# Fifteenth mixing gate ahead of the first S5 states, one input product ahead of the first S5 output and a third one behind the last

## The chip, the cores and the metric

The kernel runs on one core of one Trainium2 chip. The metric is the device time of one execution in microseconds (us), taken as the median of a few runs. A core has five engines with one in-order instruction queue each: PE (TensorE, the matrix products), DVE (VectorE), ACT (ScalarE), POOL (GpSimd) and SP (SyncE, which here only issues transfers). They wait for one another through semaphores.

## What is computed

One layer of a recurrent diffusion backbone for 128 context tokens and 512 latent tokens, 640 columns in all. Cut to what matters here:

```
hn = rmsnorm(x) * (1 + sc1) + sh1
xa, ga, xs = split(hn @ w_in, [1024, 2048])          # LRU input, LRU gate, S5 input
ua = depthwise_conv4(xa)                             # centred, per channel
r, i = sigmoid(block_diag(ua, w_r) + b_r), sigmoid(block_diag(ua, w_i) + b_i)    # per direction
ha = linear_scan(a(r), b(r, i, ua)), both directions
ya = gelu(ga) * ha
vs = gelu(S5(xs) + D * xs);  ys = vs * sigmoid(vs @ s5_w_glu + b)
gate_a, gate_b = split(sigmoid(hn @ w_gate + b_gate))
m  = (gate_a * (ya @ w_proj_lru) + gate_b * (ys @ w_proj_s5)) @ w_out
x  = x + g1 * rmsnorm(m);   then a SwiGLU feed-forward part
```

## The kernel before

Every matrix product is done in three passes over operands split into a high and a low part, so one product of a 128-column weight block with the 640 columns of `hn` is 48 matmuls (8 blocks of the inner dimension, 3 passes, 2 halves of the columns). The weights are cut into units that stand in one list. For each unit SP fetches a raw tile (`raw`, 4 buffers), ACT writes the high part (`wh`) and DVE the low part (`wl`, 3 buffers each). `use` and `split_next` do this on demand, two units ahead of the product that is being written down; the next raw tiles are fetched as `wl` frees them. So the position of a unit in the list and the position of its product in the code both set what stands where in the queues of SP, ACT and DVE.

The order of the work is written by hand; each engine executes its instructions in the order in which the Python code emits them. The stretch of this study is the middle of the layer:

- The gate loop (products 2 to 13 of `w_gate`, `gate_job`) runs on PE while DVE walks through the 64 steps of the S5 state scan (`scan_step`, tile `F`). The steps lie in a list of background jobs, and `bg_run` emits some after each gate. `mod_done` at gate 12 puts a few DVE instructions behind the scan steps that are emitted by then: the first of them writes `modT` from the PSUM tile `q_m2`.
- `gate_job(m)` is a product into the PSUM tile `q_g`, a `shift` copy, two sigmoids on ACT and a store (`gd`) that ACT issues. PSUM has four such tiles (`q`), used in turn by every product.
- After the scan, `y_states(ct)` copies states out of `F` into two `Hst` tiles (six copies on DVE, six on ACT), for one of four channel tiles `ct`. `y_mm` multiplies with them (PSUM `q_y`), `y_out` transposes (`q_yt`) and applies GeLU on ACT (tile `vs`). Between `y_mm` and `y_out` of each `ct` one product of the LRU branch stands: `lru_xa(0)`, `lru_xa(1)`, `lru_ga(0)`, `lru_ga(1)`. An `lru_xa` is followed by `lru_x`, which copies the result to a padded tile (`xap`).
- Then come four products of the S5 gate (`glu_job(0..3)`, PSUM `q_glu`, each half as long as an input product). Behind the second and the fourth the depthwise convolution of LRU block 0 and 1 is emitted on DVE (`lru_conv`, tile `u`, and its parts `uh`, `ul`). Then `softplus` (26 tiny DVE instructions on 16 columns, tile `w16`), then `lru_w(0)` and `lru_w(1)`, which split the LRU gate weights into `lwh` (ACT) and `lwl` (DVE).
- Then a loop over pairs of blocks `c` = 2, 4, 6: two input products, the LRU gate products of the two blocks before (`lru_gates`, PSUM `q_gl`, which needs `uh`, `ul`, `lwh` and `lwl`), two more products of the other half (`lru_ga`), and the LRU recurrences on ACT and DVE.

Of the kernel before, what the change touches and what calls it, by code (L numbers as in the profile page):

```python
# [18 lines left out]
KD = D // 128  # L19
# [20 lines left out]
def hybrid_step_kernel(ctx: ExitStack, tc: tile.TileContext, A, y_prompt, y_sample, o_lru, o_re, o_im):  # L40
# [23 lines left out]
    def mm(out, lhsT, rhs, start, stop):  # L64
        PE.matmul(out, lhsT=lhsT, rhs=rhs, start=start, stop=stop, skip_group_check=True)  # L65

    def psq(name):
        return ps.tile([128, 1024], F32, tag="q", name=name)

    def ttile(name, shape=(128, TW), dt=F32, pool=None):  # L70
        return (pool or tp).tile(list(shape), dt, tag="t", name=name)
# [4 lines left out]
    def bg_run(us=1e9, upto=None):  # L76

        credit[0] = us if upto or us > 1e8 else credit[0] + us
        while bg and credit[0] > 0:
            if upto and upto not in [job for _, job in bg]:  # L80
                break
            cost, job = bg.popleft()
            if callable(job):
                job()
            credit[0] -= cost
        if upto or not bg:
            credit[0] = 0.0
# [33 lines left out]
    def unit(src, shape, split=True):  # L121
        units.append({"src": src, "shape": list(shape), "split": split})
        return len(units) - 1
# [67 lines left out]
    def colmajor(w, c0, n=128):  # L191
        return w[:, c0:c0 + n].rearrange("(k p) c -> p k c", p=128)

    w_in, w_gate, w_mod = A["w_in"][0], A["w_gate"][0], A["w_mod"][0]
# [16 lines left out]
    U_XA, U_GA = [], []  # L211
    U_GLU = None
    for c in range(0, 8, 2):
        for j in range(2):
            U_XA.append(unit(colmajor(w_in, (c + j) * 128), (128, KD, 128)))
        for j in range(2):
            U_GA.append(unit(colmajor(w_in, 1024 + (c + j) * 128), (128, KD, 128)))
            if c + j == 1:
                U_GLU = [unit(w_glu[:, m * 256:m * 256 + 256].rearrange("(k p) c -> p k c", p=128), (128, 4, 256))
                         for m in range(2)]  # L220
    U_G.append(unit(colmajor(w_gate, GO[15] * 128), (128, KD, 128)))
# [100 lines left out]
    q = psq("q_c")  # L322
# [44 lines left out]
    q = psq("junk")  # L367
# [172 lines left out]
    def vec(name, i):  # L540
        o = VOFF[name] + i
        return V[:, o:o + 1]
# [95 lines left out]
    for k in range(KD + 1):  # L638
        if k < KD:
            q = psq("q_x")  # L640
# [130 lines left out]
    def seg_act(out, q, func, b):  # L771
        for s, (lo_, hi_) in enumerate(((0, NP), (NP, T))):
            act(out[:, lo_:hi_], q[:, 192 + lo_:192 + hi_], func, bias=b[:, s:s + 1])
# [17 lines left out]
    xq = [psq(f"q_xs{m}") for m in range(2)]  # L791
# [32 lines left out]
    q = psq("q_xs")  # L824
# [15 lines left out]
    def gate_mm(m):  # L840
        q = psq("q_g")
        mtile(q, wblocks(U_G[m]), hn, range(KD))
        return q

    def gate_job(m, pool=None, q=None):
        q = gate_mm(m) if q is None else q
        g = ttile("gate", pool=pool)
        seg_act(g, q, AF.Sigmoid, shift(q, vec("b_gate", GO[m])))
        if pool is None:
            ACT.dma_start(out=gd[GO[m]], in_=g[:, 0:T])  # L850
        return g[:, 0:T]
# [119 lines left out]
    def y_load(ct, half):  # L971
        tk = ttile("tk")
        g0 = 8 * ct + 4 * half
        for g in range(4):
            b = Kd[g0 + g, 0:16, 0:8 * H5]
            SP.dma_start(out=tk[:, g * 128:(g + 1) * 128],
                         in_=bass.AP(tensor=b.tensor, offset=b.offset, ap=[[H5, 8]] + list(b.ap)))
        return tk
# [8 lines left out]
    q = gate_mm(0)  # L987
# [31 lines left out]
    for m in range(2, 14):  # L1019
# [10 lines left out]
        if 5 <= m < 13:  # L1030
# [2 lines left out]
            k_stage(m - 5)  # L1033
            bg_run(2.2)
    tks = [y_load(0, 0), y_load(0, 1)]
    bg_run()


# [26 lines left out]
    def y_mm(ct, tks, Hst):  # L1065
        ysb = [ttile(f"ysb{a}") for a in range(2)]
        for half in range(2):
            tk = tks[half]
            g0 = 8 * ct + 4 * half
            q = psq("q_y")  # L1070
            for gg in range(4):
                g = g0 + gg
                o = q[0:NCH, gg * 128:(gg + 1) * 128]
                mm(o, Ug(g), tk[:, gg * 128:(gg + 1) * 128], True, False)
                for d in range(2):
                    hs = Hst[d][:, (g % 8) * NCH:(g % 8 + 1) * NCH]
                    mm(o, hs, Pt[d][:, g].rearrange("p k h -> p (k h)"), False, d == 1)
            for a in range(2):
                src = q[0:NCH, 0:512].rearrange("p (g j h) -> p j g h", g=4, j=8)[:, ::-1][:, 4 * a:4 * a + 4]
                dst = ysb[a][0:NCH, 0:512].rearrange("p (j g h) -> p j g h", j=4, g=8)[:, :, 4 * half:4 * half + 4]  # L1080
                if a:
                    act(dst, src, AF.Copy)
                else:
                    DVE.tensor_copy(out=dst, in_=src)
        return ysb
# [26 lines left out]
    def lru_xa(c):  # L1112
        q = psq("q_xa")
        mtile(q, wblocks(U_XA[c]), hn, range(KD))
        return q
# [3 lines left out]
    def lru_x(c, q):  # L1119
        x = ttile("xap", pool=lps[-1])  # L1120
        POOL.memset(x[:, 0:2], 0.0)
        POOL.memset(x[:, 130:133], 0.0)
        POOL.memset(x[:, 645:648], 0.0)
        b = shift(q)
        act(x[:, 2:130], q[:, 192:320], AF.Identity, bias=b[:, 0:1])
        act(x[:, 133:645], q[:, 320:832], AF.Identity, bias=b[:, 1:2])
        return x
# [27 lines left out]
    def lru_ga(c, ahead=2):  # L1155
        q = psq("q_ga")
        mtile(q, wblocks(U_GA[c], ahead=ahead), hn, range(KD))
        return q

    def lru_gelu(c, q):  # L1160
        g = ttile("gel")[:, 0:T]
        seg_act(g, q, AF.Gelu_apprx_tanh, shift(q))
        gel[c] = g
# [85 lines left out]
    fin = ttile("fin")  # L1249
    DVE.tensor_copy(out=fin[:, 0:64].rearrange("p (a b) -> p a b", a=2), in_=F[:, :, :, 16])  # L1250
    hst = y_states(0)
    gate_job(14)
    xs0 = []
    for ct in range(4):
        ysb = y_mm(ct, tks, hst)
        if ct == 0:
            q = psq("q_ns")
            transpose(q[0:64, 0:128], fin[:, 0:64])
            fo = ttile("fin")
            DVE.tensor_copy(out=fo[0:64, 0:128], in_=q[0:64, 0:128])  # L1260
            SP.dma_start(out=o_re[0, 0].rearrange("d (g a) p -> (d g) (a p)", a=2), in_=fo[0:32, 0:128])
            SP.dma_start(out=o_im[0, 0].rearrange("d (g a) p -> (d g) (a p)", a=2), in_=fo[32:64, 0:128])
        if ct < 3:
            tks = [y_load(ct + 1, 0), y_load(ct + 1, 1)]
            hst = y_states(ct + 1)
        xq = lru_xa(ct) if ct < 2 else lru_ga(ct - 2)
        y_out(ct, ysb)
        if ct < 2:
            xs0.append(lru_x(ct, xq))
        else:  # L1270
            lru_gelu(ct - 2, xq)
    fp.__exit__(None, None, None)
    s5p.__exit__(None, None, None)
    lpool = tc.tile_pool(name="lru", bufs=27, side="right")
# [15 lines left out]
    def glu_job(m):  # L1290
        q = psq("q_glu")
        mtile(q, wblocks(U_GLU[m // 2], 4, (m % 2) * 128), vsh, range(4))
        g = ttile("sg")[:, 0:T]
# [11 lines left out]
    for c in range(2):  # L1305
        lru_w(c)
    for c in range(2, 8, 2):
        q = lru_xa(c)
        if c > 2:
            lru_scan(c - 4)  # L1310
        xs = [lru_x(c, q)]
        q = lru_xa(c + 1)
        if c > 2:
            lru_scan(c - 3)
            lru_mul(c - 4)
            lru_mul(c - 3)
        lru_conv(c, xs[0])
        xs.append(lru_x(c + 1, q))
        lru_gates(c - 2)
        lru_gates(c - 1)  # L1320
        lru_conv(c + 1, xs[1])
        gq = [lru_ga(c)]

        def front():
            lru_iu(c - 2)
            lru_iu(c - 1)
            for j in range(2):
                lru_ul(c + j)
            for j in range(2):
                lru_w(c + j)  # L1330
            gq.append(lru_ga(c + 1, ahead=1))

        def s5_split():
            for m, g in enumerate(yf):
                yh = ttile(f"ysh{m}", dt=F32R)[:, 0:T]
                yl = ttile(f"ysl{m}", dt=F32R)[:, 0:T]
                act(yh, g, AF.Copy)
                tt(yl, g, yh, ALU.subtract)
                ys.append((yh, yl))
            split_next()  # L1340

        if c < 6:
            ta = lru_decay((c - 2, c - 1), front, split_next)
        else:
            ta = lru_decay((c - 2, c - 1), None, lambda: [front(), s5_split()])
        lru_drive(ta, (c - 2, c - 1))
        if c > 2:
            lru_split(c - 4)
            lru_split(c - 3)
        for j in range(2):  # L1350
            (lru_gelu if c < 6 else lru_raw)(c + j, gq[j])
        warm(AF.Sigmoid)
# [89 lines left out]
    for j, (part, m) in enumerate(items):  # L1442
        if j:
# [5 lines left out]
            elif part == "b":  # L1449
                for i in range(NP1):  # L1450
                    q = psq("q_pl")
# [5 lines left out]
            else:  # L1457
                q = psq("q_pl")
# [7 lines left out]
        if j == 2:  # L1466
            q = psq("q_nl")
# [86 lines left out]
    for i in range(5):  # L1554
# [3 lines left out]
        q = wo_mm(i, mid)  # L1558
# [88 lines left out]
    for k in range(KH):  # L1647
        a, b = tk[k]
        p, q = f[k], f[k + KH]
# [206 lines left out]
```

## Time and profile before

| | us |
|---|---|
| median of 3 runs | 1039.13 (1036.62 to 1042.95) |
| the profiled execution, its own time | 1037.07 |
| its span in the trace | 1035.3 |
| PE busy | 989.7 (96% of the span) |
| PE weight loads busy | 911.1 (88%) |
| DVE busy | 668.3 (65%) |
| ACT busy | 461.0 (45%) |
| POOL busy | 197.2 (19%) |

PE is the engine that is nearly always busy; the other four work beside it. The busy share is a mean over stages, so what a reordering is worth is read from the few places where PE waits, and from what ends each wait.

### The profile page before, as it was taken

The page shows a single profiled execution, that of the slowest core. Times are in us where ns is not written, and L with a number is a line of the kernel's source. Part 1 is how long each engine was busy: PE and PEld are TensorE (multiplying, and loading weights), DVE is VectorE, ACT ScalarE, POOL GpSimd, SP SyncE. Part 2 cuts the span into 40 slices and gives each one's busy share as a digit, 9 for nine tenths or more (in the row PEclk, how much of TensorE's full clock was granted, in tenths as well). Part 3 has the DMA queues.
Part 4 walks back from the last instruction along what each step waited for, and adds up shares of the span by engine and source line. Part 5 has one row for each costly group of instructions (what it writes and reads, how often), then busy time and mean ns, then how long its engine had stood idle before and what let it go on. Part 6 is the DMA issues. An engine that isn't in the chain of part 4 may idle for free.

```text
span 1035.3 us, 16728 instructions
## 1 busy us (share of the span) xinstructions
PE 989.7 (96%) x6649; PEld 911.1 (88%) x6649; DVE 668.3 (65%) x1103; ACT 461.0 (45%) x748; POOL 197.2 (19%) x200
## 2 busy tenths in 40 slices
PE   5999999979999999999999989999999999999997
PEld 3698988879999999987877889999999999888885
DVE  5789899962477989782575785555555565434113
ACT  5535423234349889732242443444454454333112
POOL 4000000000000000300310274555555551000002
PEclk9999999989999999999999999999999999999999
DMA  9944276543213221747562312223322223522202
GB/s 305 322 115 128 68 210 199 186 152 96 63 42 102 61 73 49 259 133 210 178 201 104 121 43 82 81 83 87 96 83 82 83 82 122 206 79 82 70 13 101
DMA packets 135901, 125.57 MB, mean 121 GB/s; under 512 B 17320, under 2 KB 115384, under 8 KB 135824
## 3 DMA queue, kind: packets, MB, share of 16 engines
q1 hardware_dynamic: 129888, 111.82, 35.1%
q10 hardware_dynamic: 4080, 7.31, 2.1%
q0 software_dynamic: 1856, 5.38, 1.5%
q8 instruction: 52, 0.85, 0.3%
q14 instruction: 25, 0.20, 0.1%
HBM read 111.63 MB, written 12.85 MB: 120 GB/s over the span
## 4 chain that ended last, share of the span: by engine, by line
PE 73%; DVE 15%; ACT 5%; DMA 3%; issue 2%; SPq 0%; POOL 0%; ACTq 0%; DVEq 0%
PE f L65 15%; PE ffX L65 13%; PE q_g L65 6%; PE ffY L65 6%; PE q_pl L65 6%; PE q_xa L65 4%; PE q_wo L65 3%; PE ffZ L65 3%; PE q_ga L65 3%; DVE wl L59 2%; PE q_ff L65 2%; PE q_y L65 2%; PE q_m L65 2%; PE q_gl L65 2%; DVE F L59 2%
## 5 line engine op out<-in xcount | busy, mean ns | idle before, releaser
L59 DVE TENSOR_TENSOR wl<-raw,wh 128x1024 fp32r<-128x1024 f32 (+1 forms) x104 | 126.5, 1221 | 148.9 <-ACT wh L62 148.7
L62 ACT ACTIVATE wh<-raw 128x1024 fp32r<-128x1024 f32 (+1 forms) x106 | 110.5, 1047 | 180.2 <-PE f L65 81.9
L59 DVE TENSOR_TENSOR wl<-s,wh 128x1024 fp32r<-128x1024 f32 x38 | 55.1, 1450 | 60.8 <-ACT wh L62 60.8
L65 PE MATMUL f<-wl,ah 128*128 128x512 f32 x220 | 87.1, 396 | 0.0
L65 PE MATMUL f<-wh,ah 128*128 128x512 f32 x220 | 87.1, 396 | 0.0
L65 PE MATMUL f<-wh,al 128*128 128x512 f32 x220 | 87.1, 396 | 0.0
L65 PE MATMUL q_g<-hnh,wh 128*128 128x320 f32 (+1 forms) x256 | 60.8, 319 | 5.5 <-ACT Hst L62 5.5
L59 POOL TENSOR_TENSOR s<-raw 128x512 f32<-128x512 f32 x38 | 52.6, 1384 | 58.1 <-DVE wl L59 30.0
L65 PE MATMUL q_g<-hnl,wh 128*128 128x320 f32 (+1 forms) x256 | 59.4, 313 | 0.0
L65 PE MATMUL q_g<-hnh,wl 128*128 128x320 f32 (+1 forms) x256 | 59.3, 314 | 0.0
L65 PEld LDWEIGHTS f<-wl,ah 128*128 128x128 f32 x220 | 41.5, 188 | 9.9
L65 PEld LDWEIGHTS f<-wh,al 128*128 128x128 f32 x220 | 41.4, 188 | 10.0
L65 PEld LDWEIGHTS f<-wh,ah 128*128 128x128 f32 x220 | 41.4, 188 | 9.9
L65 PEld LDWEIGHTS q_g<-hnh,wh 128*128 128x128 f32 x256 | 43.5, 192 | 6.9 <-ACT Hst L62 5.7
L65 PE MATMUL ffX<-Th,wh 128*128 128x320 f32 x152 | 47.0, 310 | 0.0
L65 PE MATMUL ffX<-Tl,wh 128*128 128x320 f32 x152 | 47.0, 310 | 0.0
L65 PE MATMUL ffX<-Th,wl 128*128 128x320 f32 x152 | 47.0, 309 | 0.0
L62 ACT ACTIVATE u<-ffX 128x320 f32<-128x320 f32 x38 | 16.6, 438 | 64.3 <-PE ffX L65 64.3
L62 ACT ACTIVATE wh<-s 128x1024 fp32r<-128x1024 f32 x38 | 39.8, 1048 | 11.4 <-PE q_ff L65 6.0
L65 PEld LDWEIGHTS q_g<-hnl,wh 128*128 128x128 f32 x256 | 43.8, 192 | 0.0
L65 PEld LDWEIGHTS q_g<-hnh,wl 128*128 128x128 f32 x256 | 43.8, 191 | 0.0
L59 DVE TENSOR_TENSOR F<-F,sc 128x64 f32<-128x64 f32 (+1 forms) x128 | 39.5, 308 | 3.8
(388 smaller groups left out, 2803.9 us busy)
## 6 DMA issues: line engine op xcount, KB each, us to landing
raw<-in_w_ff_in SPq DMA_DIRECT2D x44, 512.0 KB
raw<-in_w_mod SPq DMA_DIRECT2D x32, 512.0 KB
raw<-in_w_ff_out SPq DMA_DIRECT2D x22, 512.0 KB
raw<-in_w_in SPq DMA_DIRECT2D x20, 512.0 KB
raw<-in_w_gate SPq DMA_DIRECT2D x16, 512.0 KB
wm<-in_w_mod SPq DMA_DIRECT2D x12, 512.0 KB
gd<-gate ACTq DMA_DIRECT2D x16, 320.0 KB
raw<-in_w_out SPq DMA_DIRECT2D x8, 512.0 KB
```

The source lines that it names most:

```text
L59: (eng or DVE).tensor_tensor(out=out, in0=a, in1=b, op=op)
L62: ACT.activation(out=out, in_=in_, func=func, **kw)
L65: PE.matmul(out, lhsT=lhsT, rhs=rhs, start=start, stop=stop, skip_group_check=True)
```

## The change

The product of gate 14, with its evacuation, is emitted before the background list is run empty and so before the copy `fin` and `y_states(0)`; it stood behind both. The first input product, `lru_xa(0)` with `lru_x(0)`, moves from between `y_mm(0)` and `y_out(0)` to the place ahead of `y_mm(0)`. Its old place takes `lru_xa(1)`, and `lru_ga(0)` and `lru_ga(1)` move up by one `ct` each. The last place, between `y_mm(3)` and `y_out(3)`, takes `lru_xa(2)`, which was the first product behind the four of the S5 gate. The list of weight units follows: the unit of `lru_xa(2)` now stands ahead of the two of the S5 gate.

```diff
@@ -211,11 +211,12 @@
     for c in range(0, 8, 2):
-        for j in range(2):
+        for j in range(1 if c == 2 else 0, 2):
             U_XA.append(unit(colmajor(w_in, (c + j) * 128), (128, KD, 128)))
         for j in range(2):
             U_GA.append(unit(colmajor(w_in, 1024 + (c + j) * 128), (128, KD, 128)))
             if c + j == 1:
+                U_XA.append(unit(colmajor(w_in, 2 * 128), (128, KD, 128)))
                 U_GLU = [unit(w_glu[:, m * 256:m * 256 + 256].rearrange("(k p) c -> p k c", p=128), (128, 4, 256))
                          for m in range(2)]
@@ -1033,6 +1034,7 @@
     tks = [y_load(0, 0), y_load(0, 1)]
+    gate_job(14)
     bg_run()
@@ -1249,9 +1251,11 @@
     hst = y_states(0)
-    gate_job(14)
     xs0 = []
     for ct in range(4):
+        if ct == 0:
+            xq = lru_xa(0)
+            xs0.append(lru_x(0, xq))
         ysb = y_mm(ct, tks, hst)
@@ -1263,12 +1267,12 @@
-        xq = lru_xa(ct) if ct < 2 else lru_ga(ct - 2)
+        xq = lru_ga(ct - 1) if 0 < ct < 3 else lru_xa(1 if ct == 0 else 2)
         y_out(ct, ysb)
-        if ct < 2:
-            xs0.append(lru_x(ct, xq))
+        if 0 < ct < 3:
+            lru_gelu(ct - 1, xq)
         else:
-            lru_gelu(ct - 2, xq)
+            xs0.append(lru_x(1 if ct == 0 else 2, xq))
@@ -1305,10 +1309,12 @@
     for c in range(2, 8, 2):
-        q = lru_xa(c)
-        if c > 2:
+        if c == 2:
+            xs = [xs0[2]]
+        else:
+            q = lru_xa(c)
             lru_scan(c - 4)
-        xs = [lru_x(c, q)]
+            xs = [lru_x(c, q)]
```

On ACT, around the first states of the S5 outputs (`Hst`, read from the scan's tile `F`), the queue before is this; the store in the first row is that of gate 13:

```order
L850 DMA gd<-gate 128x640
L62 ACTIVATE Hst_2595<-F 64x4x81 x2
L62 ACTIVATE Hst_2600<-F 64x4x16
L62 ACTIVATE Hst_2600<-F 64x4x64
L62 ACTIVATE Hst_2600<-F 64x4x16
L62 ACTIVATE Hst_2600<-F 64x4x64
L62 ACTIVATE wh<-raw 128x1024
L62 ACTIVATE shift<-q_g,V 128x2
L62 ACTIVATE gate<-q_g,shift 128x128
L62 ACTIVATE gate<-q_g,shift 128x512
L850 DMA gd<-gate 128x640
```

The same place of the changed kernel, from the store of gate 13 on:

```order
L851 DMA gd<-gate 128x640
L62 ACTIVATE wh<-raw 128x1024
L62 ACTIVATE shift<-q_g,V 128x2
L62 ACTIVATE gate<-q_g,shift 128x128
L62 ACTIVATE gate<-q_g,shift 128x512
L851 DMA gd<-gate 128x640
L62 ACTIVATE Hst_2656<-F 64x4x81 x2
L62 ACTIVATE Hst_2661<-F 64x4x16
L62 ACTIVATE Hst_2661<-F 64x4x64
L62 ACTIVATE Hst_2661<-F 64x4x16
L62 ACTIVATE Hst_2661<-F 64x4x64
```

The evacuation of gate 14 (`shift`, two `gate`) now stands ahead of the six `Hst` copies, which therefore come after the product of gate 14 is done.

On DVE, the queue from the second S5 gate (`sg`) to the first convolution (`u`) and past it, before and after, is the same row for row up to the end of `softplus`. Behind `softplus` stand the low parts of the LRU gate weights (`lwl`), the low parts of weight units (`wl`) and the convolutions of blocks 2 and 3 (`u`). Before:

```order
L732 TENSOR_SCALAR sp<-w_3349 128x16
L59 TENSOR_TENSOR lwl<-lw_3179,lwh 128x512
L59 TENSOR_TENSOR lwl<-lw_3185,lwh 128x512
L59 TENSOR_TENSOR wl<-raw,wh 128x1024 x2
L1131 TENSOR_SCALAR u<-xap,V 128x644
```

After:

```order
L733 TENSOR_SCALAR sp<-w_3412 128x16
L59 TENSOR_TENSOR lwl<-lw_3242,lwh 128x512
L59 TENSOR_TENSOR lwl<-lw_3248,lwh 128x512
L59 TENSOR_TENSOR wl<-raw,wh 128x1024
L1133 TENSOR_SCALAR u<-xap,V 128x644
```

One `wl` fewer stands between `lwl` and the convolution of block 2; that unit's split has moved up, the order of everything ahead of `lwl` is unchanged. On PE the four S5 gate products are followed by the LRU gate products (`q_gl`) with 96 rows of `q_xa` between them before, and 48 after; both kernels have the same instructions in total.

## Rows read from the trace of the kernel before

**Rows 1.** Waits view of PE: engine and line waited for; us in total, times, longest.

```profile
PE q_g L65 <- ACT Hst L62: 5.5, 1, 5.5
...
PE q_pl L65 <- DVE plp L59: 3.2, 1, 3.2
...
PE q_m L65 <- DVE gld L59: 1.8, 1, 1.8
...
PE q_gl L65 <- ACT gate L62: 1.6, 1, 1.6
...
PE q_gl L65 <- ACT ri L62: 1.0, 1, 1.0
...
PE q_pl L65 <- DVE gld L59: 0.6, 1, 0.6
```

**Rows 2.** Timeline of DVE, scan's end: start, us, instruction, tiles, shapes, count, [idle before].

```profile
220.11 0.59 DVE L59 TENSOR_TENSOR F<-F,sc 128x64 f32<-128x64 f32 x2
220.61 0.18 DVE L59 TENSOR_TENSOR modT<-q_m,bmt 128x32 f32<-128x32 f32 x1
```

**Rows 3.** Timeline of PE, product of gate 14: its start, and the change of pace.

```profile
220.93 0.87 PE L65 MATMUL q_g<-hnh,wh 128*128 128x320 f32 x2 [5.47 <-ACT Hst L62]
...
225.15 0.46 PE L65 MATMUL q_g<-hnh,wl 128*128 128x320 f32 x2
...
227.52 0.46 PE L65 MATMUL q_g<-hnl,wh 128*128 128x320 f32 x2
```

**Rows 4.** Timeline of ACT: first states, and the evacuation of gate 14.

```profile
219.88 2.13 ACT L62 ACTIVATE Hst<-F 64x324 f32<-64x324 f32 x6 [3.13 <-DVE F L59]
...
230.40 0.94 ACT L62 ACTIVATE gate<-q_g,shift 128x128 f32<-128x128 f32 x2
231.38 0.33 ACTq L850 DMA_DIRECT2D gd<-gate  x1
```

**Rows 5.** Chain that ended last, in order of time: start, us, what.

```profile
220.93 9.14 PE q_g L65 x48
230.07 5.24 PE q_y L65 x48
...
235.42 7.12 PE q_xa L65 x48
...
281.87 14.12 PE q_glu L65 x96
295.99 14.25 PE q_xa L65 x96
310.24 7.12 PE q_gl L65 x48
317.35 14.22 PE q_ga L65 x96
331.57 14.27 PE q_xa L65 x96
345.84 7.19 PE q_gl L65 x48
```

**Rows 6.** Timeline of ACT: second S5 gate.

```profile
289.00 0.80 ACT L62 ACTIVATE sg<-q_glu,V 128x640 f32<-128x640 f32 x1 [2.15 <-PE q_glu L65]
```

**Rows 7.** Timeline of DVE: second S5 gate, low parts, next units, next convolution.

```profile
289.82 0.82 DVE L59 TENSOR_TENSOR sg<-sg,vs 128x640 f32<-128x640 f32 x1 [2.12 <-ACT sg L62]
...
308.39 1.29 DVE L59 TENSOR_TENSOR lwl<-lw,lwh 128x512 fp32r<-128x512 f32 x2
309.60 2.35 DVE L59 TENSOR_TENSOR wl<-raw,wh 128x1024 fp32r<-128x1024 f32 x2
```

**Rows 8.** Waits view of DVE, from 284 to 320 us.

```profile
DVE ul L59 <- ACT uh L62: 1.7, 2, 0.9
```

**Rows 9.** Timeline of PE: first LRU gate product.

```profile
310.07 0.46 PE L65 MATMUL q_gl<-uh,lwh 128*128 128x322 f32 x2
310.37 0.46 PE L65 MATMUL q_gl<-uh,lwl 128*128 128x322 f32 x2
```

**Rows 10.** Timeline of PE behind two shorter waits.

```profile
453.30 0.64 PE L65 MATMUL q_pl<-yah,wh 128*128 128x320 f32 x2 [0.63 <-DVE gld L59]
...
457.26 0.46 PE L65 MATMUL q_pl<-yah,wl 128*128 128x320 f32 x2
```

**Rows 11.** Busy time by stretch: us, PE, PEld, DVE, ACT, POOL, then PEclk, DMA, GB/s.

```profile
221.00:225.00 4.00, 4.00 (x16) 4.00 (x16) 3.84 (x11) 2.05 (x5) 0.22 (x3) 0.51 0.14 36
...
230.00:282.00 52.00, 52.00 (x420) 51.97 (x419) 17.05 (x39) 21.50 (x50) 0.66 (x11) 1.00 0.32 92
```

## The prediction

> **What bounds the kernel now.** I read the table of busy times first: PE is busy for 96% of the span, so only its idle places can give anything. The waits view of PE then lists them. Inside the stretch that the change reorders there is one, of 5.5 us, ahead of gate 14's product [rows 1]. The chain that ended last runs on PE without a gap from there to the second pair of LRU gate products at 345.84 us [rows 5]. Behind it, until about 453 us, the chain is one of ACT and DVE work (the LRU recurrences), and PE waits there five more times, 8.2 us in all (3.2, 1.8, 1.6, 1.0 and 0.6) [rows 1].
>
> Next I asked what ends the 5.5 us wait, since the change is built around it. The waits view names an `Hst` copy on ACT. But the product of gate 14 reads no `Hst`. What it needs and gets last is its PSUM tile: it takes the one that `q_m2` held, and that is read by the DVE instruction that writes `modT`. This stands behind the last scan steps on DVE. The timeline bears that out: `modT` runs from 220.61 for 0.18 us, so to 220.79, and PE starts at 220.93 [rows 2, 3]. The scan, one step behind the other on DVE, ends this wait, and the ACT copy ran beside it by chance.
>
> **The change, part by part.**
>
> *Gate 14 emitted earlier.* On PE nothing changes: gate 14 follows gate 13 in both kernels, takes the same PSUM tile, and waits for the same `modT`, which stands behind the same scan steps. All scan steps are already emitted when the loop ends, so the closing `bg_run` has none left to put behind it. Worth: 0 of the 5.5 us. On ACT the six `Hst` copies now queue behind gate 14's evacuation, which cannot start before that product ends. The evacuation's sigmoids start at 230.40 and its store is issued at 231.38, 0.33 us long; the copies take 2.13 us [rows 4], so they are done at about 231.7 + 2.1 = 233.8 instead of 222.0. In the old order that would have held up the first S5 output, which starts at 230.07 [rows 5], by 3.8 us.
>
> *First input product ahead of the first S5 output.* It is what covers those 3.8 us. It takes 7.12 us [rows 5] and needs nothing from the scan, so the first S5 output starts at 230.07 + 7.12 = 237.2, 3.4 us after the last `Hst` copy. Cost 0, gain 0: PE had no gap here either.
>
> *The products moved up, and the third one behind the last output.* Between two S5 outputs one product of the same length stands, as before; each of the four outputs, its transposes, its copies and its table loads shift by 7.12 us. Weights: every unit keeps its lead of two products, and its transfer is issued no later relative to its product than before. So the S5 gate products, at 281.87 before [rows 5], start at 289.0. Cost up to here 0.
>
> *What no longer stands behind the S5 gate products.* Here the change costs. Before, PE had two input products (14.25 us) between the S5 gate products and the first LRU gate product [rows 5]; now it has one. That LRU gate product therefore stands where it stood, at 310.1 us: 7.12 later for the shift, 7.12 earlier for the missing product. But its operand `lwl` comes from a DVE queue that starts from the S5 gate products, and they are 7.12 us later. Follow it: the second S5 gate on ACT starts at 289.00, released by PE [rows 6]; the DVE multiplication behind it at 289.82 [rows 7]. From there DVE goes through convolution 0, two more gates, convolution 1 and `softplus`, all in the old order, and starts the two `lwl` at 308.39. They take 1.29 us, so the first is done at about 308.39 + 0.65 = 309.04 [rows 7]. PE reads it first at 310.37 [rows 9], a margin of 1.33 us. All of this DVE work moves by 7.12 us, PE's reading does not. The first `lwl` is done at 316.2, and PE waits 7.12 - 1.33 = 5.8 us between the first and the second pair of matmuls of that product. `lwl` of the next block follows 0.65 us later and is needed 3.6 us later, so it adds nothing. The bounds: on the way DVE idles only for two `uh` copies of ACT, 1.7 us in all [rows 8]; if both vanished, the wait would be 4.1; an upper bound is the whole shift, 7.1. I take 5.8, since the order on both engines is the old one.
>
> *The clock.* After the 5.47 us wait at gate 14 the granted clock was 0.51 in the stretch from 221 to 225, that is the 1.2 GHz level, against 1.00 from 230 to 282 [rows 11]. The first eight pairs of matmuls took 225.15 - 220.93 = 4.22 us, the next eight 227.52 - 225.15 = 2.37 us [rows 3]: 1.85 us lost. Behind the shorter waits around 450 us eight pairs took 457.26 - 453.30 = 3.96 us [rows 10], 1.6 lost at the same pace. The new wait is as long as the one at gate 14, so I take 1.85; bounds 0 (clock kept) and, if both LRU gate products ran slowly from end to end, their 7.12 us [rows 5] once more.
>
> The Trainium skill, in TensorE: Matmul & The Clock Gate, section Terms, prices a throttled stretch as its length times the part of the pulses that is withheld. For 4.22 us at half clock that is an estimate of 2.1 us, by which the sum below would be 7.9 us instead of 7.65. The trace's 1.85 us stands, as its first and last pair lie across the change of level.
>
> *What follows.* From the stall to the second pair of LRU gate products PE does the same work as before without a gap, so these end 7.65 us later. DVE is 7.12 us later, less the one `wl` (half of 2.35 us [rows 7]) that now stands ahead of `lwl`: about 5.9, so it is not what PE waits for next. The chain of ACT and DVE work from 353 to 453 us starts from those products' results and moves with them; the five waits of PE in it keep their length, and nothing is given back.
>
> Sum: 5.8 + 1.85 = 7.65 us slower. The profiled execution took 1037.07 us (span 1035.3 and 1.8 around it), so 1044.7 on its scale. The median of the three runs shown is 2.06 us above that execution; carried to it, 1039.13 + 7.65 = 1046.8 us, 0.7% slower.
>
> **The rivals.**
>
> *Nothing changes* (1039 us, 1037 to 1041). PE's new wait is paid back later because the recurrences do not hang on it, and the 8.2 us of later waits [rows 1] shrink by as much. For it: the later waits are long enough. Against it: the chain that leads to them starts from the LRU gate products on PE, which are late.
>
> *Faster* (1031.8 us). The waits view is right and an ACT instruction behind the `Hst` copies ends the wait at gate 14. Then moving gate 14 ahead of them takes away 5.5 us and the slow start, 1.85: minus 7.3, and 1031.8 if there is also no new wait at the LRU gates; with that wait it comes to about 1039.5, no change. It decides if, in the changed kernel, PE starts gate 14 before `modT` ends. Against it: the product reads none of these tiles, and PE starts 0.14 us after `modT` [rows 2, 3].
>
> *Slower by more than 1%* (1052.1 us). The wait at the LRU gates comes, and PE stays at the low clock through both products: 5.8 + 7.12 = 12.9 us, 1039.13 + 12.9. It decides if the slow pace lasts beyond some 5 us of matmuls there. Against it: both slow stretches read here ended after about 4 us [rows 3, 10].
>
> **How the numbers follow.** Forecast 0.74; nothing changes 0.13; the wait at gate 14 gone 0.05 (0.02 of it without the new wait); low clock throughout 0.08. The forecast's own range is 4.1 (shortest wait, clock kept) to 9.0 us (7.1 and 1.85), so 1043 to 1048 us, and the runs shown scatter by 3 us to either side of their median. For 8 in 10 I reach down to the case without change and up to what scatter can add: 1038 to 1051. One per cent, about what a measurement of this kernel can tell from no change, is 10.4 us, so the line to slower is at 1049.5: reached by the low-clock case and by 0.08 of the forecast with its scatter, 0.16 together. Faster by over 1% would be under 1028.7 and even the fast rival ends above; 0.02 for that case with scatter. The rest, 0.82, is within 1%.
>
> **What would show it.** PE's wait ahead of gate 14 is still about 5.5 us and ends with `modT`. No PE wait between 230 and 310 us. A new PE wait of 4 to 7 us in the first `q_gl`, put down to DVE `lwl`, at about 310.4, with a granted clock near 0.5 for some 4 us behind it. The first pair of LRU gates ends near 325 instead of 317, and the waits from 411 on come 7 to 8 us later with their old lengths. I am wrong if `lwl` starts before 313 us, if gate 14 starts before `modT` ends, or if the later waits shrink.

## The result, and the profile after

The changed kernel takes 1044.89 us (median of 10 runs, 1041.2 to 1047.04) against 1038.52 us for the kernel before in the same comparison (10 runs, 1035.26 to 1042.95). The ratio is 1.0068, with a 95% interval from 1.0053 to 1.0084: 5.5 to 8.7 us slower. The forecast was 7.65 us slower. The profiled execution took 1044.38 us, its span 1042.6 us.

First the waits of PE in the changed kernel, as in [rows 1]: engine and line waited for, us in total, times, longest.

```profile
PE q_g L65 <- ACT wh L62: 5.7, 1, 5.7
PE q_gl L65 <- DVE lwl L59: 5.4, 1, 5.4
...
PE q_pl L65 <- DVE plp L59: 2.9, 1, 2.9
...
PE q_m L65 <- DVE gld L59: 1.8, 1, 1.8
...
PE q_gl L65 <- ACT gate L62: 1.6, 1, 1.6
...
PE q_gl L65 <- ACT ri L62: 1.0, 1, 1.0
...
PE q_pl L65 <- DVE gld L59: 0.6, 1, 0.6
```

The wait ahead of gate 14 (`q_g`) is still there, 5.7 us against 5.5. One line is new, 5.4 us for `lwl` ahead of the first LRU gate product. The five later waits add up to 7.9 us against 8.2.

What ended the wait at gate 14? The timelines of DVE, PE and ACT (start, us, engine, line, instruction, count, idle time before it) answer [rows 2 to 4]:

```profile
221.87 0.18 DVE L59 TENSOR_TENSOR modT<-q_m,bmt 128x32 f32<-128x32 f32 x1
```

```profile
222.20 0.87 PE L65 MATMUL q_g<-hnh,wh 128*128 128x320 f32 x2 [5.74 <-ACT wh L62]
...
228.18 0.46 PE L65 MATMUL q_g<-hnh,wl 128*128 128x320 f32 x2
```

```profile
221.03 1.06 ACT L62 ACTIVATE wh<-raw 128x1024 fp32r<-128x1024 f32 x1 [3.29 <-DVE F L59]
...
232.51 0.95 ACT L62 ACTIVATE gate<-q_g,shift 128x128 f32<-128x128 f32 x2
...
233.86 2.13 ACT L62 ACTIVATE Hst<-F 64x324 f32<-64x324 f32 x6 [0.40 <-ACT gate L62]
```

PE starts 0.15 us after `modT` ends (222.05). The view named `Hst` before and names `wh` now; both are ACT instructions that happened to run beside the end of the scan. The six `Hst` copies stand behind gate 14's evacuation, as worked out ahead, and are done at 235.99.

The chain that ended last shows what became of the products [rows 5]:

```profile
222.20 9.98 PE q_g L65 x48
232.18 7.13 PE q_xa L65 x48
239.31 5.24 PE q_y L65 x48
...
291.07 7.09 PE q_glu L65 x48
...
318.30 9.53 PE q_gl L65 x46
327.83 14.25 PE q_ga L65 x96
...
427.10 3.58 PE q_gl L65 x22
...
462.57 5.54 PE q_pl L65 x36
...
481.19 0.99 PE q_m L65 x8
```

The first `q_y` starts 3.3 us after the last `Hst` copy. The chain leaves PE when the S5 gate product of 291.07 ends, runs over ACT and DVE, and comes back to PE at 318.30: that is the new wait. Here it is on DVE and PE [rows 7, 9]:

```profile
317.55 1.29 DVE L59 TENSOR_TENSOR lwl<-lw,lwh 128x512 fp32r<-128x512 f32 x2
```

```profile
312.37 0.56 PE L65 MATMUL q_gl<-uh,lwh 128*128 128x322 f32 x2
318.30 0.91 PE L65 MATMUL q_gl<-uh,lwl 128*128 128x322 f32 x2 [5.37 <-DVE lwl L59]
...
323.77 0.47 PE L65 MATMUL q_gl<-ul,lwh 128*128 128x322 f32 x2
```

And the granted clock in stretches of the changed kernel (length, busy us of PE, PEld, DVE, ACT, POOL, then clock, DMA share, GB/s):

```profile
222.20:226.20 4.00, 4.00 (x15) 4.00 (x16) 3.93 (x7) 0.00 (x0) 0.17 (x3) 0.50 0.10 30
...
318.30:323.30 5.00, 5.00 (x19) 5.00 (x20) 4.83 (x7) 1.91 (x3) 0.00 (x0) 0.50 0.16 36
323.80:327.80 4.00, 4.00 (x28) 4.00 (x28) 2.75 (x4) 3.19 (x4) 0.00 (x0) 1.00 0.53 148
427.10:431.00 3.90, 3.90 (x26) 3.90 (x27) 2.33 (x4) 3.90 (x6) 0.67 (x3) 1.00 0.98 306
```

Behind each of the two long waits PE starts at the 1.2 GHz level (0.50); behind the second the next line shows it back at the full 2.4 GHz (1.00), and behind the first the stretch from 228.20 to 232.20 has 1.00 too.

The following table cuts the chain of both kernels into the same pieces of work; each was profiled a second time (below). The columns are the time from gate 14's first matmul to the next product; from the first `q_y` to the first `q_ga` behind the LRU gates (7.12 us of input product taken out for the kernel before, where that stretch holds one more); from there to the short wait of 1.0 us at `q_gl`; and from there to the first `q_pl` of 48 matmuls.

| kernel | gate 14 starts | gate 14 | S5 outputs to LRU gates | to the short wait | behind it |
|---|---|---|---|---|---|
| before | 220.93 | 9.14 | 80.16 | 99.18 | 58.49 |
| before, second profile | 221.94 | 8.95 | 80.16 | 99.17 | 57.80 |
| changed | 222.20 | 9.98 | 88.52 | 99.27 | 55.09 |
| changed, second profile | 226.22 | 9.84 | 88.40 | 99.24 | 55.08 |

So the two spans, 7.3 us apart, differ by 1.3 us ahead of gate 14, 0.8 at gate 14, 8.4 at the LRU gates, 0.1 behind them, and **minus 3.4 us** behind the short wait; 0.1 lies still later. The 1.3 us ahead are scatter (the second profile of the changed kernel starts gate 14 another 4.0 us later; one early wait, for a copy of `bmt`, is 3.8 us there and 1.1 in the first).

Where the 3.4 us lie is read from the chain of the kernel before:

```profile
416.53 4.87 PE q_gl L65 x22
...
453.30 7.07 PE q_pl L65 x36
...
473.44 1.58 PE q_m L65 x8
```

The same three pieces took 3.58, 5.54 and 0.99 us in the changed kernel. The first two differ by the clock, 2.8 us together: the granted clock was 0.70 and, in the first 4 us of the second, 0.57 before, and 1.00 in the changed kernel. The third differs by 0.6 us at a granted clock of 1.00 in both. There PE's weight loads waited for a transfer in the kernel before, which the waits view of PE does not list but that of PEld does (here from 410 to 490 us), and in the changed kernel they did not:

```profile
PEld q_m L65 <- DMA raw<-in_w_mod: 0.5, 1, 0.5
```

### The profile page after: what moved, and what is told of

It is laid out like the page before. It is cut to its first block, busy times and chain, and to the rows that moved or that the text cites. A ratio compares the mean times of both kernels' runs of the same rounds, so it can differ in the third digit from the quotient of the medians.

```text
span 1042.6 us, 16720 instructions
## 1 busy us (share of the span) xinstructions
PE 989.9 (95%) x6649; PEld 910.9 (87%) x6649; DVE 668.7 (64%) x1103; ACT 461.1 (44%) x748; POOL 198.0 (19%) x200
## 4 chain that ended last, share of the span: by engine, by line
PE 72%; DVE 15%; ACT 6%; DMA 4%; issue 2%; SPq 0%; POOL 0%; ACTq 0%; DVEq 0%
PE f L65 15%; PE ffX L65 13%; PE q_g L65 7%; PE ffY L65 6%; PE q_pl L65 5%; PE q_xa L65 3%; PE q_wo L65 3%; PE ffZ L65 3%; PE q_ga L65 3%; DVE wl L59 2%; PE q_y L65 2%; PE q_ff L65 2%; PE q_gl L65 2%; PE q_m L65 2%; DVE F L59 2%
```

## The experiments

My theory: the cost is the wait for `lwl`, made by the input product that no longer stands behind the S5 gates; gate 14's wait is ended by `modT` and is untouched. The main rivals: the cost comes from gate 14's new place; an ACT instruction ends its wait; the new wait is paid back later.

### One part undone: the third product behind the S5 gates again

The list of weight units goes back with it; that part of the edit is left out here.

```diff
-        xq = lru_ga(ct - 1) if 0 < ct < 3 else lru_xa(1 if ct == 0 else 2)
+        xq = lru_ga(ct - 1) if 0 < ct < 3 else lru_xa(1) if ct == 0 else None
...
-            xs = [xs0[2]]
+            xs = [lru_x(c, lru_xa(c))]
```

> The changed kernel with one part undone: the third input product stands behind the S5 gate products again, so two products separate these from the first LRU gate product, as in the kernel before. Gate 14 and the first input product stay where the change put them; nothing now stands between the last S5 output and its transposes. My theory (the cost is the lost product behind the S5 gates): no PE wait in the first q_gl, gate 14's wait still about 5.5 us; a new PE wait of about 1 us ahead of the last q_yt, where the copies of ysb are no longer covered; time within 2 us of before. Rival, the cost comes from gate 14 standing ahead of the states (a longer slow start, or S5 outputs that wait for Hst): the time stays 5 to 8 us above before, and the lost time shows ahead of 285 us.

Measured: 1041.79 against 1038.09 us, ratio 1.0045 (1.0026 to 1.0063), 3.7 us between the medians. The waits view:

```profile
PE q_g L65 <- DVE modT L59: 5.8, 1, 5.8
...
PE q_yt L104 <- DVE ysb L1085: 0.6, 1, 0.6
PE q_glu L65 <- PE q_yt L104: 0.6, 1, 0.6
```

And the waits of the weight loads, from 282 to 302 us:

```profile
PEld q_glu L65 <- DVE vsl L59: 1.7, 4, 0.5
```

The wait for `lwl` is gone, so the theory of its cause holds. But I missed the size of what comes in its place. The last S5 output ends at 283.39 (278.13 and 5.26) and the next input product starts at 301.36: 17.97 us, against 14.69 in the kernel before (274.18 to 295.99 less its 7.12 us gate product): 3.3 us lost behind the S5 outputs. Gate 14 took 9.33 us, against 9.14 and 8.95 in the kernel before, and the outputs took their old time, so next to nothing was lost where the rival put the cost. The product between the last output and its transposes covers more than the `ysb` copies: the first S5 gate product now meets the `vsl` splits on DVE one by one, four waits of up to 0.5 us. And the waits view of PE names `modT` at gate 14 here.

### One part alone: the third product ahead of the S5 gates, in the kernel before

The list of weight units is that of the changed kernel; that part of the edit is left out here.

```diff
             lru_gelu(ct - 2, xq)
+    xs0.append(lru_x(2, lru_xa(2)))
...
+        if c == 2:
+            xs = [xs0[2]]
+        else:
```

> The kernel before with one part of the change alone: the third input product stands between the last S5 output and the S5 gate products, instead of behind these. Gate 14 and the first two input products stand where they were. My theory: the whole cost of the change comes with this part: a PE wait of 5 to 6 us in the first q_gl, put down to DVE lwl, a slow stretch of 1.9 to 2.6 us behind it, and 6 to 8 us above before. Rival (the cost comes from gate 14's place): no more than 1 us above before.

Measured: 1046.09 against 1038.09 us, ratio 1.0083 (1.006 to 1.0107).

```profile
PE q_g L65 <- ACT Hst L62: 5.9, 1, 5.9
PE q_gl L65 <- DVE lwl L59: 5.4, 1, 5.4
```

This one edit gives the same 5.4 us wait and the whole cost, 8.0 us between the medians. Gate 14's place has little to do with it.

### The LRU weights split ahead of the softplus chain

```diff
-    softplus()
     for c in range(2):
         lru_w(c)
+    softplus()
```

> The changed kernel with one order on DVE turned round: the split of the first two LRU weight blocks (lwh, lwl) stands ahead of the softplus chain of 27 small instructions instead of behind it. In the changed kernel's trace that chain runs from 312.57 to 317.55, 5.0 us. My theory: lwl starts 5.0 us earlier, PE's wait in the first q_gl falls from 5.4 to about 0.5 us, the slow stretch behind it goes too, and the time is 5 to 8 us below the changed kernel, within 2 us of before. Rival, another operand of that product (ul, or the weights of the next unit) comes at the same time: the wait stays above 3 us and is put down to that. Rival, the wait is paid back downstream whatever its length: the time does not move.

Measured: 1038.26 against 1038.09 us, ratio 1.0007 (0.9991 to 1.0024); 6.6 us below the changed kernel's 1044.89, or 6.2 if each is set against the kernel before of its own comparison. DVE and PE at the place:

```profile
310.93 1.29 DVE L59 TENSOR_TENSOR lwl<-lw,lwh 128x512 fp32r<-128x512 f32 x2
```

```profile
311.67 0.57 PE L65 MATMUL q_gl<-uh,lwl 128*128 128x322 f32 x2 [0.38 <-DVE lwl L59]
```

The wait falls from 5.4 to 0.4 us, the 5.0 us of the chain that stood ahead of `lwl`, and the slow stretch behind it goes too. Nothing else was late at that place, and the wait was not one that is paid back whatever its length.

### modT ahead of the last scan steps, in the changed kernel

The first half of `mod_done`, which writes `modT`, becomes a function of its own:

```diff
         gate_job(m)
+        if m == 12:
+            mod_cols(1, q2)
         bg_run(6.2 + (1.4 if 4 <= m < 12 else 0))
...
-            mod_done(1, pre1, row1, q2)
+            mod_done(1, pre1, row1, q2, cols=False)
```

> The changed kernel with the one DVE instruction that writes modT moved ahead of the last scan steps, so that the PSUM tile which gate 14 takes is free early. My theory (modT ends gate 14's wait): gate 14 starts within 0.5 us of the end of gate 13, about 5.5 us earlier, without the slow stretch; the first input product covers the scan's end and the copies Hst, and no wait takes its place ahead of the S5 outputs; the wait for lwl at the first q_gl stays near 5.4 us; 7 to 9 us below the changed kernel, so within 2 us of before. Rival (an ACT instruction, Hst or wh, ends that wait, as the waits view says): gate 14 still waits more than 4 us and the time does not move. Rival (the wait moves): PE waits ahead of the first q_y instead, and less than 3 us is gained.

Measured: 1037.77 against 1038.09 us, ratio 1.0003 (0.9981 to 1.0026); 7.1 us below the changed kernel, or 6.7 in the same way. DVE, PE and SP at gate 14, and a row of the waits view:

```profile
217.55 0.18 DVE L59 TENSOR_TENSOR modT<-q_m,bmt 128x32 f32<-128x32 f32 x1
```

```profile
217.88 0.53 PE L65 MATMUL q_g<-hnh,wh 128*128 128x320 f32 x2 [0.72 <-DVE modT L59]
```

```profile
225.78 6.16 SPq L980 DMA_DIRECT2D tk<-Kd  x8
```

```profile
PE q_gl L65 <- DVE lwl L59: 5.4, 1, 5.4
```

With `modT` done at 217.73, PE starts gate 14 at 217.88 without any change on ACT. That settles the releaser: `modT`, not `Hst` or `wh`. Gate 14 takes 7.36 us instead of 9.98, the S5 outputs follow without a wait, and `lwl` costs its 5.4 us as before. So here the first input product does cover something: gate 14 ends at 225.23, the first loads of the tables `tk`, which the first S5 output reads, are issued from 225.78 on, and that output starts at 232.37.

### The same move in the kernel before

The edit is that of the run above, made in the kernel before.

> The kernel before, with modT alone moved ahead of the last scan steps: no part of the change. It asks what the first input product ahead of the first S5 output is worth as a cover once gate 14 no longer waits. My theory: gate 14 starts about 5 us earlier and at full clock; the first S5 output then waits for the Hst copies that DVE makes behind the scan's end (in the trace of before these end at 224.8, gate 14 would end at about 223.9), a new PE wait of 0.5 to 1.5 us ahead of the first q_y; no wait for lwl at the first q_gl; 5 to 7 us below before. Rival (the cover is needed for more than that): a wait above 3 us ahead of the first q_y, and less than 4 us gained.

Measured: 1038.25 against 1037.35 us, ratio 1.002 (1.0001 to 1.0039). Nothing was gained, and the forecast of this run was wrong. PE and SP show where the 5 us went:

```profile
217.87 0.53 PE L65 MATMUL q_g<-hnh,wh 128*128 128x320 f32 x2 [0.83 <-DVE modT L59]
...
230.36 0.69 PE L65 MATMUL q_y<-tk,U 128*81 128x128 f32 x2 [5.14 <-DMA tk<-Kd]
```

```profile
224.18 0.58 SPq L614 DMA_DIRECT2D gsc<-gx  x2
225.31 0.40 SPq L130 DMA_DIRECT2D raw<-in_s_w_glu  x1
225.76 5.05 SPq L979 DMA_DIRECT2D tk<-Kd  x8
```

I had followed only the `Hst` copies to the first S5 output. It also reads `tk`, and the eight `tk` loads stand on SP behind the two `gsc` stores and a weight fetch. The stores wait for `gx`, the fetch is issued when a DVE split `wl` ends at 225.29, and both DVE instructions stand behind the scan. So gate 14's wait and the loads of the first output hang on the same chain: a gate 14 that starts earlier only waits longer behind itself, and the clock falls there too (that `q_y` takes 7.77 us instead of 5.24).

### The table loads ahead of the stores

The move of the run above, and on SP's queue alone:

```diff
             mod_cols(1, q2)
+            tks = [y_load(0, 0), y_load(0, 1)]
...
-    tks = [y_load(0, 0), y_load(0, 1)]
     bg_run()
```

> The kernel before with modT moved ahead, as in the run where the wait went over to the first S5 output, and with one more move on SP's queue alone: the eight loads of tk for that output are issued ahead of the two gsc stores and of the next weight fetch, which wait for DVE instructions behind the scan's end. The instructions of the other engines are the same. My theory: in that run the first S5 output waited 5.1 us for tk because SP held the loads back until 225.8; issued at about 218 they land by about 225, and what is late next is the Hst copies on DVE, done at 226.9 against the end of gate 14 at 225.2. So the wait ahead of the first q_y falls from 5.1 to between 1.2 and 2.0 us and is put down to DVE Hst, and the time is 3 to 5 us below that run and below before. Rival, the wait was for Hst or for the weights all along: 4.5 to 5.5 us again and no gain.

Measured: 1030.70 against 1037.87 us, ratio 0.9943 (0.9924 to 0.9962): 7.2 us faster than before.

```profile
216.58 5.32 SPq L979 DMA_DIRECT2D tk<-Kd  x8
```

```profile
PE q_y L65 <- DVE Hst L1064: 0.7, 2, 0.4
```

Counted from the start of gate 14 (216.38 here, 217.87 there) the loads are issued 7.7 us earlier, the wait of 5.1 us is gone, and the `Hst` copies cost 0.7 us in two pieces: less than the 1.2 to 2.0 expected, since the first pair of `q_y` reads `tk` and no `Hst`, and the copies are then waited for one at a time. With no long wait there is no slow stretch either, which the expected 3 to 5 us had left out.

### Both moves on DVE in the changed kernel

The edits are the two shown above: `lru_w` ahead of `softplus`, and `mod_cols` ahead of the last scan steps.

> The changed kernel with both moves on DVE: modT ahead of the last scan steps, and the split of the first LRU weights ahead of the softplus chain. Each of them alone brought the changed kernel back to the time of before. My theory: the two waits are independent, since each stands ahead of its own product and the work between them moves as a whole, so both go: gate 14 waits 0.7 us, the first q_gl 0.4 us, and the time is 6 to 8 us below before. Rival (with one wait gone the other takes over what it saved, or the later waits grow): less than 3 us below before.

Measured: 1032.37 against 1037.35 us, ratio 0.9939 (0.9918 to 0.9961): 5.0 us below before between the medians, 6.3 by the ratio.

```profile
PE q_g L65 <- DVE modT L59: 0.8, 1, 0.8
...
PE q_gl L65 <- DVE lwl L59: 0.4, 1, 0.4
```

The two waits are independent; each of the moves alone took the changed kernel back to the time of before, and both together beat it. So the change's first product does what it can do once gate 14 is free, and its third product costs next to nothing (a wait of 0.4 us) once `lwl` is early. But the kernel before gained as much, 0.9943, with `modT` and the table loads moved and nothing of the change: no run here shows a gain that needs the change.

### Both kernels once more

> The changed kernel once more, unchanged, for a second profile. It asks which of the differences between the two traces belong to the change. My theory: the waits at gate 14 (5.4 to 5.9 us) and for lwl (5.4 us) are the same again; the length of the slow stretch behind each wait (2.7 us lost at gate 14 and 2.5 us at the first q_gl in the first profile) and the start of gate 13 differ by up to 1 us from execution to execution, and so does the clock in the stretches from 418 to 470 us. Rival (all of these belong to the change): the same values within 0.2 us.

> The kernel before once more, unchanged, for a second profile. My theory: gate 14's wait of 5.4 to 5.9 us and no wait for lwl again; the pace behind gate 14 and the clock in the stretches from 410 to 460 us differ by up to 1.5 us in sum from the first profile. In the first profile the q_gl behind 416 us took 4.87 us and the q_pl behind 453 us took 7.07 us, against 3.58 and 5.54 us in the changed kernel. Rival (the change itself gave these 2.8 us back): 4.87 and 7.07 us again, within 0.2 us, where the changed kernel shows 3.58 and 5.54 again.

Single executions of 1047.72 and 1037.58 us. The waits came again: 5.8 and 5.4 us in the changed kernel, 5.9 and none in the kernel before. The table above has the stretches. Of the two rivals on the gain behind the short wait, neither holds cleanly. The changed kernel showed 3.58 and 5.52 us again for the `q_gl` and the `q_pl`, the kernel before 6.29 and 5.51 instead of 4.87 and 7.07: there each varies, but the sum of the two stayed 2.7 to 2.8 us above the changed kernel's.

These two pieces differ by the clock, not by waits. This is the `q_gl` behind the short wait in the kernel before, and its second profile:

```profile
416.50:421.40 4.90, 4.87 (x24) 4.88 (x25) 2.06 (x3) 4.21 (x6) 0.71 (x2) 0.70 0.99 346
```

```profile
417.30:423.60 6.30, 6.26 (x23) 6.26 (x24) 2.07 (x3) 4.45 (x6) 0.73 (x2) 0.51 0.83 298
```

The same waits (1.6 and 1.0 us) stand ahead of it in all eleven profiles of this study. In the four with the 5.4 us wait for `lwl` 100 us earlier it took 3.55 to 3.58 us. Of the seven without it, six took 4.87 to 6.29, and one, the kernel with the early table loads, 3.55. So the wait for `lwl` goes with the full clock at this later place but isn't needed for it.

Nor does that wait bring the whole gain. This is the chain of the kernel with the third product alone, which has the wait too:

```profile
426.13 3.55 PE q_gl L65 x22
...
461.60 7.06 PE q_pl L65 x36
```

From the short wait to the first `q_pl` of 48 matmuls (the last column of the table) it took 57.69 us, about 1.0 of it a wait of PEld for a weight transfer and 1.5 the slower `q_pl`. The other three profiles with the wait for `lwl` took 55.08 or 55.09 us, the seven without it 56.59 to 58.70, three of these with such a transfer wait of 0.5. What decides the clock here I can't say, and no run shows that the change itself brings the gain.

## Why the prediction came out as it did

**Gate 14, 0 of the 5.5 us: right, and for the reason given.** The wait stayed at 5.7 us, PE started 0.15 us after `modT`, and moving `modT` alone took the wait away. What the step left out: the product behind the wait took 0.7 to 1.0 us longer in the changed kernel (9.98 and 9.84 us, against 9.14 and 8.95). In the other two kernels that have gate 14 ahead of the states and wait for `modT` it took 9.33 and 9.64 us, and with the third product alone, where gate 14 stands behind them, 9.00. Its place goes with the longer slow stretch; why stays open.

**The first input product as cover for Hst: right in its place, too narrow in its reason.** The copies ended at 235.99, the first output started at 239.31. But once gate 14 no longer waits, the same product also covers the `tk` loads, which no step named. That mattered for the rival: with gate 14's wait taken away the changed kernel gained 6.7 to 7.1 us, near the rival's 7.3, while the same removal in the kernel before was worth nothing.

**No wait between 230 and 310 us: right.** The S5 gates started at 291.07, and the S5 outputs took their old 5.24 us each.

**The new wait, 5.8 us: right.** The second pair of the first `q_gl` came 5.93 us after the first, against 0.30 before [rows 9], so PE lost 5.63 us, and 5.4 of it is shown as the wait for `lwl`. The two experiments that put that product back, or moved only it, tie the wait to the lost product; the turned order on DVE ties it to the softplus chain.

**The slow clock behind it, 1.85 us: too small.** From the first pair to the end of the product it is 327.83 - 312.37 = 15.46 us, against 7.28 before; less the 5.63, the clock took 2.55 us. In the changed kernel's second profile and the other two kernels with this wait the product was 9.40, 8.70 and 9.20 us long instead of 9.53, so it took 2.4, 1.7 and 2.2. The step had carried over the length of one slow stretch, 4.22 us; this one lasted from 318.30 to 323.77, 5.47 us. Its 1.85 us was also a little less than its own rows hold: gate 14's whole product took 9.14 us against 7.12 for an input product of as many matmuls [rows 5], 2.0 lost. The first of the eight slow pairs does not lie across the change of level, as the step has it; it took 0.67 us, the longest of them. The Trainium skill, in TensorE: Matmul & The Clock Gate, section Terms, prices a throttled stretch by its length and the withheld share of pulses; for 5.47 us at half the pulses that is an estimate of 2.7 us, near the 2.55 measured. What failed is the length, not the price. The Trainium skill, on the same page, in Part 1, says that the number of slow matmuls at the start of a kernel varies between its runs. Here, in the middle of one, the two profiles of the changed kernel bear that out only weakly: 9.53 and 9.40 us; the lower values are those of other kernels.

**Nothing is given back: wrong.** This is the step that failed. The later waits did keep their lengths (7.9 against 8.2 us), as it said. But time came back without one of those waits growing shorter: behind the short waits from 425 us on PE ran at the full clock where the kernel before ran part of that work at the lower level, 2.8 us in the first pair of profiles and 2.7 in the second. Another 0.6 us of the first pair is the transfer that only the kernel before waited for. The step looked at the waits of PE alone and put the clock behind them at no difference. Without the gain the first pair would sum to 9.3 us, above the measured 5.5 to 8.7, which speaks for some of it in most executions. Whether the change brings it stays open, since the third product alone had it only in part.

**The sum.** Predicted 5.8 + 1.85 = 7.65. The profiles show 0.8 + 8.4 + 0.1 - 3.4 = 5.9 us, and 0.9 + 8.2 + 0.1 - 2.7 = 6.5 in the second pair, without the scatter ahead of gate 14; the measured ratio stands for 5.5 to 8.7. The total came out close by luck, because the errors have opposite signs: a slow clock sized too small at two places, 1.5 us together, and a gain of 2.7 to 3.4 us that was not seen. Ahead of that gain the first error stands alone: the `q_gl` behind the short wait came 10.6 us later (427.10 against 416.53), 1.3 of it scatter, where the prediction has 7 to 8. And the comparison told 0.7% from no change, where the prediction allowed it about one per cent.

## What to carry to other kernels

A product that is moved from behind a step to ahead of it delays everything that starts from that step and leaves the next reader where it stood: compare the margin of each operand at that reader with the length of what was moved. Before a wait is moved or covered, list every operand and buffer of the product behind it, table loads on a DMA queue too: here three of them (the PSUM tile, the states, the tables) came from one scan, and freeing one showed the next. A changed order on a slower engine was the cheapest repair here: splitting the weights ahead of a chain that nobody needs yet took away 5 us of waiting.

## What the runs showed of the hardware

A wait of 1.0 us was followed by a granted clock of 0.51 over 6.3 us of matmuls in one profile (the kernel before, the second time) and by 1.00 over the same work in another (the changed kernel), with the same waits ahead of it. Behind waits of 5.1 to 5.9 us the product that followed ran slowly at first in every profile, and lost between 1.6 and 2.6 us against the same product without such a wait (7.36 us for gate 14). A loss that is carried over from one profile is therefore good to about 1 us behind the long waits here, and not to 2 us behind the short one, where the same work took 3.55 to 6.29 us.
